# Two small early stores on ScalarE's queue in place of one later store, in a 2x2x2 average pool

## The chip, the cores and the metric

One core of a Trainium2 chip. The metric is the device time of one execution in microseconds. Runs of one kernel scatter by about 0.5% (91.56 to 92.04 us in the widest series of the kernel before), and the 95% intervals of the ratios below are about 0.2% to either side, so smaller differences are not resolved. The record lists chip 2 for the first eight experiments and chip 1 for the last four (the four 4 KB stores, the three small stores, the other 2 KB, the second trace without a ScalarE store); each ratio is taken within one chip.

## The reference, cut to what matters

```python
# x: (8, 32, 32, 32, 32) float32, kernel_size = 2
window = x[:, :, d:d+2, h:h+2, w:w+2]
result[:, :, i, j, k] = np.mean(window, axis=(-3, -2, -1))   # (8, 32, 16, 16, 16)
```

33.55 MB are read, 4.19 MB written, and each input value is added once.

## The kernel before

The 256 (batch, channel) rows are two tiles t = 0, 1 of 128 partitions. A tile has four units of 32 KB per partition; units one to eight below count through both tiles. SyncE loads a unit, VectorE reduces it with three operations to 4 KB per partition of `obuf[t]`, and the stores carry `obuf` out. In the code `kb` counts pieces of 1 KB per partition, for loads and stores alike. Five buffers let the loads run far ahead.

```python
plan = [                        # (tile, start, pieces of the load)
    (0, 0, (32,)), (0, 32, (32,)), (0, 64, (32,)), (0, 96, (32,)),
    (1, 0, (32,)), (1, 32, (32,)), (1, 64, (16, 16)), (1, 96, (16, 16)),
]
...
for t, k0, parts in plan:       # each unit: load(s) on SyncE, then the adds
    ...
    nc.sync.dma_start(out=v, in_=xv[t*P:(t+1)*P, (k0+o)*KF:(k0+o+kb)*KF])
    ...
    pool_unit(v, t, k, kb)      # tensor_add, tensor_add, tensor_tensor_reduce
...
for queue, t, k0, kb in [       # stores: queue, tile, start, KB per partition
    (nc.scalar, 1, 0, 2),       # from the fifth unit
    (nc.sync, 0, 0, 16),
    (nc.sync, 1, 2, 12),
    (nc.sync, 1, 14, 2),        # from the last half unit
]:
    queue.dma_start(out=ov[...], in_=obuf[t][:, k0*KF:(k0+kb)*KF])
```

SyncE's stores stand behind all the loads on the same queue. The ScalarE store has a queue of its own, so it goes among the loads as soon as its unit is done.

## Time and profile before

| | before |
|---|---|
| time, median of the first three runs | 91.75 us |
| span (first to last instruction) | 86.6 us |
| last load landed | 81.15 us |
| VectorE's last instruction ends | 85.46 us |
| last store landed | 90.37 us |

The prediction says what comes after the span's end. Landings are the times at which all of a transfer's completion counts had arrived, from the trace; times within a trace count from the span's start. The lines of the page are in the prediction.

### The profile page before, as it was taken

What the parts mean: (1) busy time and instruction counts of PE and PEld (TensorE: products, weight loads), DVE (VectorE), ACT (ScalarE), POOL (GpSimd) and SP (SyncE); (2) the same over time, 40 slices, a digit from 0 to 9 for tenths busy, and PEclk for the clock granted to TensorE, in tenths of its full rate; (3) what the DMA queues carried; (4) which work ended last, traced back from release to release, by engine and by line L of the source; (5) the groups of instructions that cost most, each with busy time, mean ns of one, the idle gap of its engine ahead of it and who ended that gap; (6) DMA issues with size and microseconds to landing.
All of it is one profiled execution on the core that took longest, in us unless ns stands there. A gap on an engine that the chain in (4) does not pass through costs nothing.

```text
span 86.6 us, 91 instructions
## 1 busy us (share of the span) xinstructions
DVE 64.1 (74%) x40; POOL 0.2 (0%) x4
## 2 busy tenths in 40 slices
DVE  0000049993999749992999749992999999999994
POOL 0000000000000000000000000000000000000000
DMA  8889998899979999799988999699999999999999
GB/s 242 379 363 469 485 485 348 379 485 485 469 333 409 485 485 424 318 469 485 485 348 379 485 485 469 288 454 416 405 407 424 407 462 394 462 394 454 394 454 398
DMA packets 1774, 36.48 MB, mean 421 GB/s; under 512 B 192, under 2 KB 192, under 8 KB 320
## 3 DMA queue, kind: packets, MB, share of 16 engines
q1 hardware_dynamic: 1630, 36.22, 98.4%
q10 hardware_dynamic: 144, 0.26, 0.8%
HBM read 33.55 MB, written 4.19 MB: 436 GB/s over the span
## 4 chain that ended last, share of the span: by engine, by line
DMA 83%; DVE 14%; SPq 1%; issue 0%; DVEq 0%
DMA tin<-in_x_dram 83%; DVE tin L58 8%; DVE tin L62 4%; DVE obuf L65 2%; SPq L77 1%; DVE dummy L65 0%; DVEq L102 0%
## 5 line engine op out<-in xcount | busy, mean ns | idle before, releaser
L58 DVE TENSOR_TENSOR tin<-tin 128x4096 f32<-128x4096 f32 (+1 forms) x10 | 35.7, 3570 | 20.7 <-DMA tin<-in_x_dram 20.6
L62 DVE TENSOR_TENSOR tin<-tin 128x2048 f32<-128x2048 f32 (+1 forms) x10 | 18.6, 1865 | 0.3
L65 DVE CUSTOM_DVE_ANT_1 obuf<-tin 128x1024 f32<-128x1024 f32 (+1 forms) x10 | 10.1, 1011 | 0.3
L65 DVE DVE_READ_ACCUMULATOR2_ANT dummy<- 128x1 f32 x10 | 0.8, 82 | 0.0
L178 POOL MEMSET const-uint8-127<- 128x1 uint8 x1 | 0.1, 102 | 0.0
L178 POOL MEMSET const-bfloat16-1.0<- 128x1 bf16 x1 | 0.1, 101 | 0.0
L178 POOL MEMSET const-float32-0.0<- 128x1 f32 x1 | 0.1, 98 | 0.2 <-issue 0.2
L178 POOL MEMSET const-float32-1.0<- 128x1 f32 x1 | 0.1, 98 | 0.0
## 6 DMA issues: line engine op xcount, KB each, us to landing
tin<-in_x_dram SPq DMA_DIRECT2D x6, 4096.0 KB, 35.0
tin<-in_x_dram SPq DMA_DIRECT2D x4, 2048.0 KB, 38.9
out_dram<-obuf SPq DMA_DIRECT2D x1, 2048.0 KB, 36.8
out_dram<-obuf SPq DMA_DIRECT2D x1, 1536.0 KB, 8.8
out_dram<-obuf ACTq DMA_DIRECT2D x1, 256.0 KB, 9.9
out_dram<-obuf SPq DMA_DIRECT2D x1, 256.0 KB, 4.9
```

The lines of the kernel that those rows point to most:

```text
L58: nc.vector.tensor_add(out=b.rearrange("p (o e) -> p o e", o=od), in0=a[:, :, 0], in1=a[:, :, 1])
L62: nc.vector.tensor_add(out=c, in0=bv[:, :, 0], in1=bv[:, :, 1])
L65: nc.vector.tensor_tensor_reduce(out=obuf[t][:, o0:o0 + od * 256].rearrange("p (j k) -> p j k", k=16), in0=cv[:, :, 0], in1=cv[:, :, 1], s ...
L77: nc.sync.dma_start(out=v, in_=xv[t * P:(t + 1) * P, (k0 + o) * KF:(k0 + o + kb) * KF])
L178: nc = _bacc.Bacc("TRN2", target_bir_lowering=False, num_devices=1)
```

## The change

Its intent is to give the DMA engines some of the store traffic early, in two places, and leave less of it for the end. The bytes are the same. There is one store more.

```diff
     for queue, t, k0, kb in [
-        (nc.scalar, 1, 0, 2),
-        (nc.sync, 0, 0, 16),
-        (nc.sync, 1, 2, 12),
+        (nc.scalar, 0, 0, 2),
+        (nc.scalar, 0, 14, 2),
+        (nc.sync, 0, 2, 12),
+        (nc.sync, 1, 0, 14),
         (nc.sync, 1, 14, 2),
     ]:
```

## The prediction

> **What bounds the kernel now.** I read the page first (span, busy shares, chain), then the waits, the timeline of the tail, and last a table of windows cut at the landings of the loads. The page of the kernel before:
>
> ```profile
> span 86.6 us, 91 instructions
> DVE 64.1 (74%) x40; POOL 0.2 (0%) x4
> ...
> HBM read 33.55 MB, written 4.19 MB: 436 GB/s over the span
> ...
> DMA 83%; DVE 14%; SPq 1%; issue 0%; DVEq 0%
> ```
>
> VectorE is busy for 64.1 us only, and the chain that ended last is 83% DMA. The span ends with the last instruction, not the last byte: by the packet records the last store lands at 90.4 us, 3.8 us after the span's end and 1.4 us short of the 91.75 us measured. I predict that landing and add the same 1.4.
>
> The table of windows, one row from landing to landing (columns: stretch, its length, VectorE busy, POOL busy, clock, DMA share, GB/s):
>
> ```profile
> 21.81:31.53 9.72, 7.95 (x4) 0.00 (x0) 1.00 1.00 432
> 31.53:41.25 9.72, 7.95 (x5) 0.00 (x0) 1.00 1.00 432
> ...
> 60.67:81.15 20.48, 20.16 (x16) 0.00 (x0) 1.00 1.01 423
> 81.15:86.56 5.41, 4.22 (x4) 0.00 (x0) 1.00 0.97 413
> ```
>
> A unit of 4.19 MB lands every 9.71 us, at 432 GB/s with the DMA share at 1.00: the DMA engines never rest. VectorE needs 8.0 us of each 9.71. The row 60.67 to 81.15 holds two units and the one ScalarE store, and is 20.48 us instead of 2 x 9.71 = 19.42. After 81.15 the same engines drain the stores. The waits agree (engine, what for: total us, times, longest):
>
> ```profile
> DVE tin L58 <- DMA tin<-in_x_dram: 20.6, 6, 12.1
> ```
>
> 12.1 us of it is the first load, five more waits of 1.7 us follow, and then none over 0.2: from 60.67 VectorE has work without a break, because it falls behind in the last two units, which come as halves. The timeline (start, length, instruction):
>
> ```profile
> 59.01 0.38 ACTq L92 DMA_DIRECT2D out_dram<-obuf  x1
> 60.67 4.43 DVE L58 TENSOR_TENSOR tin<-tin 128x4096 f32<-128x4096 f32 x1 [1.69 <-DMA tin<-in_x_dram]
> ...
> 81.18 2.29 DVE L58 TENSOR_TENSOR tin<-tin 128x2048 f32<-128x2048 f32 x1
> 83.50 1.23 DVE L62 TENSOR_TENSOR tin<-tin 128x1024 f32<-128x1024 f32 x1
> 84.76 0.69 DVE L65 CUSTOM_DVE_ANT_1 obuf<-tin 128x512 f32<-128x512 f32 x1
> ```
>
> The last half unit is landed at 81.15, VectorE is free for it at 81.03: the two chains meet within 0.12 us. VectorE ends at 85.46, the last store (256 KB) is issued at 85.5, but its packets only run when the stores before it on SyncE's queue are through. By the landings in the trace: 16 KB per partition at 86.07 (4.9 us after the last load), 12 KB at 89.86 (3.8 later), the last 2 KB at 90.37 (0.5 later). So **the end is set by the sum of all DMA work on 16 engines**, with VectorE close behind.
>
> **What the Trainium skill says.** "DMA: Bandwidth & Descriptors", section "Queues, rings and completion order": each DMA engine takes packets from the queues in turn, one queue after the other. The trace agrees: the ScalarE store of 256 KB needed 9.9 us from issue to landing, because its eight 2 KB packets per engine went one by one between load packets. Same page, "Issuing engines are not separate DMA queues": a second issuing engine brings no bandwidth; the row with the store shows that, 423 GB/s instead of 432. Same page, "Where 436 GB/s comes from": a ceiling of 435 GB/s on the SBUF side, and 432 here is at it (the lower figure of about 358 per core that it gives for HBM does not bind here). "VectorE: DVE Perf Modes" gives (N+151)/0.96 ns for an fp32 tensor_tensor: 4424 ns for N = 4096, and the trace has 4426; nothing on VectorE changes.
>
> **The change, part by part.** The bytes stay: 4.19 MB of stores, the same loads, the same VectorE work. The number of stores goes from four to five.
> 1. Store of 2 KB per partition on ScalarE: one before (at 59.0, after the fifth unit), two after, free to go at about 20.1 (first unit done) and 50 (fourth unit done). What one costs among the loads: 20.48 - 19.42 = 1.06. The split of the last two units takes part of that: the last two half loads, with no store beside them, landed 4.87 and 4.95 us after the one before, against 9.71/2 = 4.855, 0.11 in sum. That leaves 0.95 us per such store. In packets: 8 per engine, 0.95/8 = 119 ns each, where a 2 KB packet records 84 ns, and 1/16 of a 32 KB load packet (1213 ns) is 76 ns. So **+0.95 us** in the load phase, of which I count none as hidden.
> 2. Store of t=0: from 16 to 12 KB per partition. The first measured 4.9 us (8 packets of 611 ns each per engine), the second costs 8 x 460 ns = 3.7: **-1.2 us**.
> 3. Store of t=1: from 12 to 14 KB per partition, estimated at 8 x 535 ns = 4.3 against 3.7: **+0.6 us**.
> 4. The last 2 KB store stays.
> Sum: 0.95 - 1.2 + 0.6 = 0.35, and with the third digits kept (4.89, 3.68, 4.28) 0.34: **+0.3 us**, wholly overhead of small packets between large ones, as the bytes cancel. The two ScalarE issues (0.38 us each) are on an idle sequencer.
>
> Does the rest keep up? The first store pushes units 3 to 8 back by 0.95, the second pushes units 6 to 8. With 7/8 of the second ahead of its landing, unit 6 comes at 60.65 + 0.95 + 0.8 = 62.4. VectorE's unbroken stretch from there to the end of the seventh half was 81.03 - 60.67 = 20.36, so it is free at 82.8, later than the last load (81.15 + 0.95 = 82.1). It ends at 82.8 + 4.3 = 87.1 against 85.46, a delay of 1.6 us. An issue took 1.0 us to its first packet on an empty queue (first load), so the last store could flow from 88.1. The stores ahead of it are through at about 89.86 + 0.34 = 90.2, on the fastest engine some 0.6 earlier. The delay is eaten by 1.4 us of spare time. The 14 KB store is issued at 82.8, can flow from 83.8, and the 12 KB store before it lasts to 82.1 + 3.7 = 85.8: no gap either.
>
> **Rivals.**
> (a) The extra store is hidden, or costs its bytes only (8 x 76 to 84 ns, so 0.61 to 0.67). It would then go between 32 KB packets, not 16 KB ones as now, and the engines might overlap such a pair better. Then the sum is 0 to +0.05: 91.75 to 91.8. Against it: the one case measured cost more than its packets' own time.
> (b) VectorE becomes the bound of the tail: if both stores delay unit 6 by more than I think, the queue runs dry before the last store. It takes over 1.4 us more delay than the 1.6 worked out; then the end is VectorE's end + 1.0 + 0.7 + completion, and each further us counts in full: 92.5 to 93. For it: the two chains meet within 0.12 us now.
> (c) A gain, because 0.26 MB less is left after the last load and the tail shrinks from 9.2 us to about 8.6. The tail is indeed shorter by 0.6, but the loads end 0.95 later. It becomes a gain only if stores among loads were nearly free, at most -0.6: 91.2.
>
> **Range and chances.** 91.75 + 0.3 = 92.05. The low end, 91.7, is rival (a) with a run's scatter (91.72 to 91.87 before); the high end, 92.5, is 1.4 us per small store or a little of (b). 2% is 1.8 us: a gain of that would need three times the store's bytes to vanish, so 0.01; a loss of that needs (b) in full, 0.03; within 2%, 0.96.
>
> **What the profile after would show.** Right: VectorE's first adds of units 4 and 5 about 0.9 us later than 41.25 and 50.96 (step 1), unit 6 at about 62.4, VectorE's end near 87.1, the DMA share at 1.0 up to the end, ScalarE stores of some 10 us each from issue to landing. Wrong in step 1 if those units come 0.6 later or not at all. Rival (b) would show as a drop of the DMA share just ahead of the last store, and a last store that lands under 3 us after its issue. The prediction also fails if the compiler's semaphores make a ScalarE store wait for something later than its own unit.

## The result, and the profile after

The changed kernel took 91.91 us (median of 6 runs, 91.68 to 92.19) beside 91.81 us (6 runs, 91.72 to 91.97) for the kernel before. The ratio is 1.0009, with a 95% interval of 0.9989 to 1.0029: the same. A ratio here is the mean time of one kernel's fast runs over that of the other's of the same rounds, so it is not quite the ratio of the medians.

From the page of the changed kernel:

```profile
span 87.6 us, 93 instructions
DVE 64.0 (73%) x40; POOL 0.2 (0%) x4
...
DMA 61%; DVE 37%; issue 0%; DVEq 0%
...
out_dram<-obuf ACTq DMA_DIRECT2D x2, 256.0 KB, 13.8
out_dram<-obuf SPq DMA_DIRECT2D x1, 256.0 KB, 4.2
```

The span grew by a whole microsecond and the share of VectorE in the chain from 14% to 37%. Neither is a loss. The span ends with the issue of the last store, and that issue moved by 0.9 us; the store then landed 4.2 us after it, in place of 4.9. The chain follows instructions, so it now turns into VectorE's unbroken stretch in the tail. What ends the kernel, the drain of the stores, lies behind both.

The windows of the changed kernel, cut at the landings (columns as in the prediction's table):

```profile
21.73:32.05 10.32, 7.95 (x5) 0.00 (x0) 1.00 1.01 431
32.05:41.80 9.75, 7.95 (x4) 0.00 (x0) 1.00 1.00 431
41.80:51.50 9.70, 7.95 (x4) 0.00 (x0) 1.00 1.00 432
51.50:61.80 10.30, 7.95 (x4) 0.00 (x0) 1.00 0.95 406
61.80:82.03 20.23, 20.02 (x15) 0.00 (x0) 1.00 1.01 422
```

The two rows that are longer than 9.71 are those with a ScalarE store beside the loads, by 0.61 and 0.59 us; the load after each takes another 0.04 or so. In the first of them 431 GB/s still move: the store's bytes are in the figure, and it is as high as in a row with loads alone. (A row's GB/s also depends on how packets fall across its edges, so the lengths are the safer reading.) The timeline shows the same from VectorE's side (start, length, instruction, idle time before it):

```profile
32.05 4.43 DVE L58 TENSOR_TENSOR tin<-tin 128x4096 f32<-128x4096 f32 x1 [2.31 <-DMA tin<-in_x_dram]
41.80 4.43 DVE L58 TENSOR_TENSOR tin<-tin 128x4096 f32<-128x4096 f32 x1 [1.74 <-DMA tin<-in_x_dram]
...
61.80 4.42 DVE L58 TENSOR_TENSOR tin<-tin 128x4096 f32<-128x4096 f32 x1 [2.29 <-DMA tin<-in_x_dram]
...
82.08 2.29 DVE L58 TENSOR_TENSOR tin<-tin 128x2048 f32<-128x2048 f32 x1
```

Two of the waits are 2.3 us instead of 1.7. So a store cost some 0.6 us here, not the 0.95. Yet the last load landed 0.88 us later than before (82.03 against 81.15), and 0.59 of it came in the last half load, which has no store beside it: it landed 5.54 us after the one before, against 4.95 in the kernel before, and other half loads need 4.89. That was the first question for the experiments.

The trace has one more thing that the diff does not show. SyncE's queue of the changed kernel (who waited for what: total us, times, longest us):

```profile
SPq L77 <- DMA tin<-in_x_dram: 10.7, 2, 9.3
SPq L77 <- DMA out_dram<-obuf: 3.9, 1, 3.9
```

A load now waits for a store to land. The two use the same semaphore in the program as compiled: the store's increment was given the semaphore that a later load takes again. It cost nothing here, because that load is issued at 40.1 us, where its buffer holds it back anyway (39.6 before), and it lands at 76.5, behind the loads queued ahead of it.

### The profile page after: what moved, and what is told of

It is laid out like the page before. It is cut to its first block, busy times and chain, and to the rows that moved or that the text cites. A ratio compares the mean times of both kernels' runs of the same rounds, so it can differ in the third digit from the quotient of the medians.

```text
span 87.6 us, 93 instructions
## 1 busy us (share of the span) xinstructions
DVE 64.0 (73%) x40; POOL 0.2 (0%) x4
## 4 chain that ended last, share of the span: by engine, by line
DMA 61%; DVE 37%; issue 0%; DVEq 0%
DMA tin<-in_x_dram 61%; DVE tin L58 20%; DVE tin L62 11%; DVE obuf L65 6%; DVE dummy L65 0%; DVEq L103 0%
```

## The experiments

Three theories of what a small ScalarE store costs while loads run:

1. **The recorded one:** 0.95 us, that is 0.34 more than its bytes need elsewhere.
2. **Its packets' own time:** 8 packets of 84 ns per engine, 0.67 us, and nothing else. The rest of the 0.95 was a stretch of slow load packets that happened to lie beside it.
3. **Hidden:** nothing.

All outputs were correct. Cuts with - and + are against the changed kernel, unless they say otherwise; where a cut has no -, it is the whole list of stores, and + marks what the kernel before does not have. The delay of a store is read from landings: the time over which the loads beside it landed, less 9.71 us per whole unit and 4.89 per half. For the changed kernel's first store, units three and four: (41.78 - 21.70) - 2 x 9.71 = 0.66.

### No ScalarE store

```diff
-        (nc.scalar, 0, 0, 2),
-        (nc.scalar, 0, 14, 2),
-        (nc.sync, 0, 2, 12),
+        (nc.sync, 0, 0, 16),
```

> No store on ScalarE: three stores on SyncE of 16, 14 and 2 KB per partition. Theory 1 (the recorded one: a small store among the loads costs 0.95 us): -0.95 + 0.6 = -0.35 us against the kernel before, ratio 0.996. Theory 2 (it costs only its packets' own time, 8 x 84 ns = 0.67 us, and the rest of the 0.95 was a stall of the transfers that happened to fall there): -0.67 + 0.61 = -0.06 us, ratio 0.999. Theory 3 (it is hidden): +0.6 us, ratio 1.0066. Landings: units at a pace of 9.7 us throughout; a stretch of slow load packets of 0.3 to 0.5 us may still be found somewhere by theory 2, not by theory 1.

91.89 us (6 runs) against 91.89 (11 runs), ratio 1.0006 (0.9987 to 1.0025). Theory 3 (1.0066) is out, and so is theory 1 (0.996). Landings went at 9.71 up to 60.6 us. The windows from there, cut at the half loads:

```profile
60.58:70.38 9.80, 9.74 (x4) 0.00 (x0) 1.00 1.01 428
70.38:75.28 4.90, 4.83 (x7) 0.00 (x0) 1.00 1.01 431
75.28:80.68 5.40, 5.30 (x6) 0.00 (x0) 1.00 1.03 407
80.68:85.60 4.92, 4.42 (x6) 0.00 (x0) 1.00 0.99 424
```

The second last row is half a unit that took 5.40 us, at 407 GB/s, without any store beside it. The slow stretch exists without stores on ScalarE. This kernel was run once more for its trace:

> The kernel with no ScalarE store, unaltered. Slow load packets near 78 us again (0.45 us per engine in the first trace) if they belong to the loads and not to any store; elsewhere or absent if they come by chance.

One run, 91.79 us. It was run on another chip. The slow stretch came back at the same place (that half unit took 5.19 us, with 0.34 us per engine of packet time beyond the usual 611 ns, in packets that began between 78 and 80 us). No ScalarE store is needed for it.

### One of the two stores alone

```diff
# first_only                      # fourth_only
+ (nc.scalar, 0, 0, 2),           + (nc.scalar, 0, 14, 2),
+ (nc.sync, 0, 2, 14),            + (nc.sync, 0, 0, 14),
+ (nc.sync, 1, 0, 14),            + (nc.sync, 1, 0, 14),
  (nc.sync, 1, 14, 2),              (nc.sync, 1, 14, 2),
```

> One ScalarE store, from the first unit; SyncE stores of 14, 14 and 2 KB per partition. Same number of small stores as before, so theories 1 and 2 both say no change in time (ratio 1.000, within 0.2%). They differ in the landings: theory 1 wants the third and fourth unit 0.95 us late in sum against a pace of 9.71, theory 2 0.6 to 0.67, theory 3 0.

> One ScalarE store, from the fourth unit; SyncE stores of 14, 14 and 2 KB per partition. Time as before by theories 1 and 2 (ratio 1.000). Landings: the sixth unit and the half after it late by 0.95 in sum (theory 1), 0.6 to 0.67 (theory 2), 0 (theory 3).

91.99 us, ratio 1.0021 (1.0000 to 1.0042), and 91.97 us, ratio 1.0016 (0.9996 to 1.0036). Both theories expected no change, so the times tell little; the landings do. The store from the first unit delayed the loads by 0.60 us, that from the fourth by 0.73, a little over theory 2's range and with 0.23 us per engine of slow load packets beside it. Neither is near 0.95.

### The changed kernel once more

> The changed kernel, unaltered. Theory 1: +0.34 us, ratio 1.0037. Theory 2: +0.06 us, ratio 1.0007. Theory 3: 0.993. Its trace also tells whether the last half load is again 0.65 us late (5.54 us after the one before, in place of 4.87): if the lateness is due to the store layout it comes back there, if it is a stall that comes and goes it is elsewhere or absent.

91.87 us (6 runs), ratio 1.0005 (0.9986 to 1.0023). The stores cost 0.61 and 0.79 us. The last half load took 5.07 us, so 0.18 over the usual in place of 0.65: the slow stretch near 78 us is there again, but its size varies from run to run.

### Other neighbours, other sizes

Units three and six split into halves, so that both stores alternate with 16 KB load packets as in the kernel before; and, in another kernel, both stores of 4 KB:

```diff
# halves_beside                           # whole_units
-        (0, 64, (32,)),                  -        (nc.scalar, 0, 0, 2),
+        (0, 64, (16, 16)),               -        (nc.scalar, 0, 14, 2),
-        (1, 32, (32,)),                  -        (nc.sync, 0, 2, 12),
+        (1, 32, (16, 16)),               +        (nc.scalar, 0, 0, 4),
                                          +        (nc.scalar, 0, 12, 4),
                                          +        (nc.sync, 0, 4, 8),
```

> The changed kernel with the third and the sixth unit loaded and reduced as two halves, so that each ScalarE store alternates with 16 KB load packets, as the one of the kernel before does. If the 0.95 us was the price beside 16 KB packets, each store now delays the loads beside it by 0.95 us; by theory 2 again by 0.6 to 0.67. Time: 0.6 us more than the changed kernel by the first, the same within 0.2% by theory 2.

> The two ScalarE stores carry 4 KB per partition, SyncE 8, 14 and 2 KB. Theory 2: the cost is the packets' own time, 8 x about 160 ns = 1.28 us per store, and the time stays as in the changed kernel (within 0.2%). Theory 1 (0.34 us overhead per store on top of its bytes): 1.55 us per store, time still +0.34 us over the kernel before. Theory 3: nothing in the landings, 1.2 us faster than the changed kernel.

Halves beside the stores: 91.75 us, ratio 0.9995 (0.9974 to 1.0017), delays (32.06 - 21.59) - 2 x 4.89 = 0.69 and 0.61. So 16 KB neighbours are not what made the store of the kernel before dear. Stores of 4 KB: 91.76 us, ratio 0.9994 (0.9973 to 1.0015), delays 1.35 and 1.59, the second with 0.37 us per engine of slow load packets near it; eight packets of 159 ns are 1.27. The time is the same in both, as theory 2 says.

### The store from the fifth unit

Why 0.95 in the kernel before? Its second trace, a kernel with another 2 KB of the fifth unit in that place, and one with all three stores:

```diff
# fifth_only_other                # three_small
+ (nc.scalar, 1, 2, 2),           + (nc.scalar, 0, 0, 2),
  (nc.sync, 0, 0, 16),            + (nc.scalar, 0, 14, 2),
+ (nc.sync, 1, 0, 2),               (nc.scalar, 1, 0, 2),
+ (nc.sync, 1, 4, 10),            + (nc.sync, 0, 2, 12),
  (nc.sync, 1, 14, 2),              (nc.sync, 1, 2, 12),
                                    (nc.sync, 1, 14, 2),
```

> The kernel before, unaltered, for a second trace. By theory 2 the two half units beside its ScalarE store are late by 0.6 to 0.67 in sum, and a stall of slow load packets of 0.2 to 0.5 us shows at some other time, as in the five other traces (near 78 us). By theory 1 they are again late by 0.95.

> One ScalarE store from the fifth unit as in the kernel before, but of other 2 KB (the second part of the unit). Slow load packets of 0.3 to 0.4 us near 61 again, and hardly any near 78, if it is the time of this store that places them; near 78 if not.

> The two ScalarE stores of the changed kernel and that of the kernel before (from the fifth unit); SyncE 12, 12 and 2 KB. Theory 2: each delays the loads beside it by 0.62, time as the changed kernel within 0.2%. Theory 1: +0.68 us over the kernel before, ratio 1.0075. If the store from the fifth unit brings its own slow load packets (0.3 to 0.4 us near 61), they show here too; if there is one such stall per run whatever the stores do, there is none near 78 then.

Before again: one run, 91.68 us; the two half loads beside the store were late by (71.38 - 60.57) - 2 x 4.89 = 1.03 in sum (the first trace by the same sum: 0.90). So its expectation from theory 2, 0.6 to 0.67, missed: the dear place is real and comes back. The other 2 KB in that place: 91.71 us, one run, late by 0.87. It was run on another chip. Its windows, half load by half load:

```profile
60.57:66.12 5.55, 5.49 (x2) 0.00 (x0) 1.00 0.99 396
66.12:71.22 5.10, 5.10 (x5) 0.00 (x0) 1.00 1.03 439
71.22:76.09 4.87, 4.77 (x6) 0.00 (x0) 1.00 1.01 431
76.09:81.07 4.98, 4.80 (x6) 0.00 (x0) 1.00 1.02 431
```

The lateness is in the first two rows, and hardly any is left in the last, where the kernel without a ScalarE store has its slow half. The packet records say what it consists of: the store's packets take 84 ns each as in the traces above, but the load packets that begin between 60 and 64 us, the first of them before any packet of the store, take up to 0.16 us more than the usual 611 ns.

The time these slow packets cost, summed over the trace from 12 us on and divided by 16 engines, is 0.43 to 0.69 us with none to three stores on ScalarE, but not with four:

| kernel | ScalarE stores | slow packets, us per engine | most of it at |
|---|---|---|---|
| no ScalarE store, two traces | 0 | 0.59, 0.50 | 76 to 80 us |
| before, two traces | 1 (fifth unit) | 0.48, 0.58 | 60 to 64 us |
| other 2 KB of the fifth unit | 1 (fifth unit) | 0.47 | 60 to 64 us |
| first, fourth unit alone | 1 | 0.60, 0.69 | 76 to 80 us |
| changed, two traces | 2 | 0.63, 0.43 | 78 to 80 us |
| halves beside the stores | 2 | 0.45 | 78 to 80 us |
| two stores of 4 KB | 2 | 0.53 | 52 to 60 us |
| three small stores | 3 | 0.45 | 58 to 65 us and 78 to 81 us |
| four stores of 4 KB (below) | 4 | 0.12 | 28 to 30 us |

The kernel with eight stores (below), whose loads came late, is left out: it has 1.26. The kernel with three stores (91.80 us, ratio 1.0000, 0.9979 to 1.0020) had some at both places; theory 1 wanted 1.0075. It was run on another chip. With a store from the fifth unit alone the slow packets come near 61 us and few are left near 78. Whether it is the same delay, pulled forward, is not shown: four 4 KB stores have hardly any, and the packets look different (up to 0.21 us over the usual near 61 us in the kernel before, up to 0.59 near 78 us in that without a ScalarE store). What slows the load packets, and what places them, no run settles; it stays open.

What the records do settle is the price of a store. Take from each delay the slow load packets that began between the landings it is read from. The twelve 2 KB stores that can be read alone, those from the fifth unit among them, are then at 0.50 to 0.64 us, mean 0.59 (kernel before: 0.90 - 0.30 = 0.60 and 1.03 - 0.41 = 0.62), and both 4 KB stores at 1.21. Their bytes need 0.61 and 1.21 us at 432 GB/s.

### Many stores: is there a limit?

> All of t=0 goes as eight 2 KB stores on ScalarE, two per unit; SyncE keeps 14 and 2 KB. Sixty-four small packets per engine then alternate with the load packets from the third unit on. Against the kernel with no ScalarE store the last load should land later by 8 x 0.62 = 5.0 us (theory 2, own time), 8 x 0.95 = 7.6 us (theory 1) or not at all (theory 3). Whole units then land at a pace of 10.3 us (theory 2) or 10.66 (theory 1). It also overruns the spare time of VectorE's tail (rival b of the prediction): by theory 2 the last load lands at about 85.5, VectorE ends 4.3 later, at 89.8, the queue is empty by then, and the last store lands 1.8 after its issue, at about 91.7 against 90.4: ratio about 1.014. Theory 1: 1.04. Theory 3: 0.97.

```diff
-        (nc.scalar, 0, 0, 2),
-        (nc.scalar, 0, 14, 2),
-        (nc.sync, 0, 2, 12),
+        (nc.scalar, 0, 2 * i, 2) for i in 0..7      # eight lines, written short
```

96.08 us, ratio 1.0465 (1.0444 to 1.0487): near theory 1's 1.04, and for another reason. The first 16 store packets per engine cost what theory 2 says: units three and four landed after 10.29 and 10.34 us. Then the loads themselves ran dry. SyncE's waits in this kernel:

```profile
SPq L77 <- DMA out_dram<-obuf: 51.7, 3, 32.1
```

With eight stores, the fifth load shares a semaphore with the first store, so it was issued at 34.3 us, after that store had landed, instead of at about 2. The next one followed at 54.0, behind another store's landing, when the fifth had already landed (53.7) and no load was queued. VectorE waited 6.2 us for unit six, against 1.7 in the kernel before, and at the end there was no store to send until VectorE had caught up: the DMA share was 0.28 from 87.46 to 89.40 us. The harmless wait of the changed kernel is the same thing at one store. This run measured the late loads, not the price of a small store, and its bearing on theories 1 and 2 ends with unit four. The same bytes in four stores, which leave the first five loads free:

```diff
# against the kernel with eight stores
-        (nc.scalar, 0, 2 * i, 2) for i in 0..7
+        (nc.scalar, 0, 4 * i, 4) for i in 0..3
```

> All of t=0 on ScalarE, as four stores of 4 KB per partition, one per unit: the same 2.1 MB among the loads as with eight small stores, but with semaphores so shared that no load has to be issued late. Theory 2 (own time, 8 x 155 ns = 1.24 us per store): units three to six land at a pace of 10.95 us in place of 9.71, the sixth at about 65.5, the last load at 85.6; VectorE is then the bound of the tail, ends at 90.2, the stores run dry, and the last store lands about 1.8 us after its issue, at 92.1 against 90.4: ratio 1.019 (rival b of the prediction). If the 1.047 of the eight small stores was due to their small packets and not to the late loads, this one stays under 1.03 all the same. Theory 3: 0.97.

93.57 us (5 runs) against 91.76 (9 runs), ratio 1.0206 (1.0182 to 1.0230), as worked out. They were run on another chip. Up to the first half after unit six the loads came (70.44 - 21.87) - (4 x 9.71 + 4.89) = 4.84 us late, 1.21 per store: the price of 0.52 MB at 432 GB/s, with no overhead to be seen. And now the tail has a hole. Windows after the last load (landed at 85.1):

```profile
85.60:87.00 1.40, 1.40 (x3) 0.00 (x0) 1.00 0.39 164
87.00:89.00 2.00, 1.97 (x2) 0.00 (x0) 1.00 1.08 452
89.00:91.27 2.27, 0.98 (x3) 0.00 (x0) 1.00 0.84 347
```

VectorE finished the seventh half at 85.8, so no store was there to fill the queue, and the DMA share fell to 0.39. The last store, issued after VectorE's end at 90.0, landed at 92.18, 1.8 us later than the 90.37 of before: that is the whole loss (1.8 us of 91.76).

## Why the prediction was right or wrong

**What bounds the kernel: right.** With none, one, two or three small stores on ScalarE the last store landed between 90.3 and 90.6 us. The sum of the DMA work ends the kernel. The 1.4 us from that landing to the measured time also held (90.58 and 91.97 in the profiled run of the changed kernel).

**Step 1, +0.95 us for a small store among the loads: wrong in size.** Eight such delays beside units three, four and six, in five traces of four kernels, were 0.60 to 0.79 us, mean 0.67 as they stand and 0.59 without the slow load packets beside them; the bytes need 0.61. I had the 0.95 from a single store in a single trace, by taking the whole lateness of two half loads as its price. Some 0.3 of it were slow load packets (0.30 us per engine in that trace), and the kernel without a ScalarE store has 0.37 to 0.45 us of them at 76 to 80 us.

**Steps 2 and 3, -1.2 and +0.6: right.** The store of t=0 took 3.67 us, from landing to landing, in place of 4.92, and that of t=1 4.33 in place of 3.79.

**The sum, +0.3: too large.** With 0.67 in step 1 it is 0.67 - 0.61 = +0.06 us. Measured: 1.0009 and 1.0005, that is +0.08 and +0.05 us, neither told apart from zero. The first interval ends at 1.0029, just below the predicted 1.0037. The forecast time of 92.05 was 0.14 us over the measured 91.91, and part of that closeness is luck: the kernel before measured 91.81 beside it, not the 91.75 from which I started. The range and the 0.96 for "same" held.

**Does the rest keep up: right, with room over.** Unit six came at 61.8, not 62.4, and VectorE ended at 86.35, not 87.1; both are mostly step 1's error carried on. The last half load at 82.03 looks like the 82.1 that I gave, but by accident: two smaller delays and a slow stretch made it up. The units four and five came 0.55 later, which is nearest to what I had named as the sign of a wrong step 1. One sign missed: the ScalarE stores took 14.4 and 13.1 us from issue to landing, not some 10. That figure came from a store between 16 KB load packets (611 ns); these wait a 32 KB one (1213 ns) out at each turn, and with 16 KB packets beside them they took 9.4 and 9.6 us.

**Rivals.** (a), that it costs its bytes only, is what happened, but not for the reason given there: between 16 KB packets a store cost no more. (b), VectorE's end as the bound, did not happen here, and the four 4 KB stores show that it is real and sized as I said: VectorE ended 4.5 us later than in the kernel before, past the 3.0 us that (b) allows, and the queue ran dry. With two 4 KB stores it ended 2.5 us later and nothing was lost. (c), hidden stores, is refuted by every landing beside one. The warning about semaphores pointed the wrong way: not a store waited for something late, but a load for a store.

No version beat the kernel before beyond the scatter. All orders of the stores with the queue kept full end within 0.3% of each other (ratios 0.9994 to 1.0021), and the one without a ScalarE store is the simplest.

## What to carry to other kernels

When the DMA engines are busy from end to end, moving a store from the end to the middle moves the loads back by the same amount; it can pay only if the engines idle somewhere, so look for a hole in the DMA share first (no run here had one to fill). Before you take a delay in one trace as the price of the operation beside it, look whether kernels without that operation have the same delay elsewhere. After adding a transfer, look at the waits of the queue that issues the loads: a shared semaphore can hold back a load that has nothing to do with it, and it costs nothing only as long as enough loads are queued.

## What the Trainium skill lacked or had wrong

- "DMA: Bandwidth & Descriptors", section "Why small descriptors are slow (HBM only)": it gives a fixed overhead of about 3 cycles per packet. With the 32 B per cycle and 850 MHz of the section "Where 436 GB/s comes from", packets of 2, 4, 12, 16 and 32 KB would move their bytes in 75.3, 150.6, 451.8, 602.4 and 1204.7 ns. The records have 84, 159, 460, 611 and 1213: 8 to 9 ns more at each of these sizes, some 7 cycles, if a record's length is the time that the page means.
- The same page, section "Queues, rings and completion order": the queues take turns as it says, but with one record a turn (a store's eight 2 KB records per engine ran spread over 62.64 to 67.86 us), where it has 9 to 17 descriptors in a typical packet, if a record is a descriptor; and it does not say how long a second queue waits for its first turn. Behind 32 KB load packets the first packet of the ScalarE store ran 3.4 us after its issue began (20.07 to 23.51); on the idle queue at the start the first load packet ran after 1.0 us.
- No page found tells of the slow load packets: 0.43 to 0.69 us per engine and run with none to three ScalarE stores, mostly near 78 us, near 61 us when a store from the fifth unit alone is among the loads, and 0.12 us with four 4 KB stores.
- Two transfers on one semaphore are told of as a danger to the data; no page found warns of the time that it can cost when a load comes to share one with a store: three waits of SyncE's loads for stores, 51.7 us in sum, in the kernel with eight stores.
